# Gate and up of a SwiGLU by Strassen's scheme in seven products, with a fixed order of three engines, and moving operands 256 bytes modulo 512 from weights

## The chip, the core and the metric

The kernel runs on one core of a Trainium2 chip. Times are microseconds (us) of one execution on the device. The kernel before took 1472.33 us, the median of three runs (1470.74 to 1473.45). The engines are TensorE (PE: matmuls; PEld: its weight loads), VectorE (DVE), ScalarE (ACT), GpSimd (POOL) and SyncE (SP, which issues DMAs).

## What is computed

A trunk of two layers over 512 tokens of 1024 features: attention and a SwiGLU feed-forward (FFN) of 2816 hidden features in each, then a last RMS norm. The change is to the two FFNs, cut here to what matters:

```python
def swiglu(h, w_gate, w_up, w_down):
    return (jax.nn.silu(h @ w_gate) * (h @ w_up)) @ w_down

for i in range(DEPTH):
    h = rmsnorm(x, norm_mix[i])
    x = x + attention_i(h)
    h = rmsnorm(x, norm_ffn[i])
    x = x + swiglu(h, w_gate[i], w_up[i], w_down[i])
return rmsnorm(x, norm_final)
```

All of it is float32. A matmul of two float32 operands is made of three fp32r matmuls: each operand is split in a high part (rounded by ACT) and a low part (what is left, by DVE), and high x high, high x low and low x high are added up in PSUM.

## The kernel before

`x` lies in SBUF transposed, features on partitions: 8 tiles (`NK`) of 128 x 512 tokens. `xh` and `xl` are the split input of the stage at hand. Weights come from `wunits`, units of 128 x 1024 floats (512 KB), eight blocks of 128 x 128. `load_unit` issues the DMA on SP into `wraw` and splits it: ACT makes `wh`, DVE makes `wl` (L92, L93). `mm3` (L113 to L119) issues the three products of one block in two halves of 256 tokens, so every matmul has a stationary operand of 128 x 128 and a moving one of 128 x 256: six per block, 48 per unit.

`swiglu` (L495 to L558) runs over 22 hidden blocks f (`NF`). For each, `gate(f)` and `up(f)` are a unit of 48 matmuls each, into PSUM banks `mm`, `sc` and `tp`. `combine(f)` scales both by the RMS norm's row `rb`, applies Silu to the gate, multiplies, and splits the product into `ah[:, f]` and `al[:, f]`. In the first f, `norm_sums` (sums over features, by one-column matmuls) stands between gate and up, and `norm_rows` (transposes into `rrow`, copied to `rb`) behind up. Then the down projection: 8 output blocks j, each of 22 x 6 matmuls with three weight loads. Behind each block comes `residual` (layer 0: adds to `x`, splits the next stage's input, and squares it), or the add, squares and a scaling by GpSimd (layer 1). The last block of layer 1 goes through `final` (L453 to L493): its two token halves are done apart, so that the norm of the first half is worked out while the second half's matmuls run. `sums(0)` is called after 6 of 22 steps of the second half, `leave(0)` after 13.

The order on PE is the order of the program's text (`manual_schedule` for PE). DVE, ACT and the others are put in order by a scheduler. `wpool` holds three sets of weight tiles, so loads run ahead. SBUF addresses come from the pools in order of their tiles. In the program as built, weight tiles start at 0 modulo 512 bytes, and `xh`, `xl`, `ah`, `al`, `oh` and `ol` at 192. In the value projections (PSUM tile `psv`) the roles are exchanged: the weights move and the input is stationary.

Of the kernel before, what the change touches and what calls it, by code (L numbers as in the profile page):

```python
# [14 lines left out]
S = 512  # L15
# [3 lines left out]
H = 16  # L19
# [4 lines left out]
WIN_A = 128  # L24
SLOPES = [float(np.float32(2.0) ** np.float32(-8.0 * (h + 1) / H)) for h in range(H)]
# [39 lines left out]
def trunk(ctx, tc, xT, gains, sink, tabs, qsc, wunits, wv, outT):  # L65
# [6 lines left out]
    spool = ctx.enter_context(tc.tile_pool(name="spool", bufs=2))  # L72
    psum = ctx.enter_context(tc.tile_pool(name="psum", bufs=2, space=bass.MemoryType.PSUM))
# [10 lines left out]
    sink_sb = const.tile([128, H], F32, name="sink_sb")  # L84
# [213 lines left out]
    with tc.tile_pool(name="l0", bufs=2) as pool:  # L298
# [14 lines left out]
        def q_unit(P, i, **kw):  # L313
            def done(ps):
                t = spool.tile([128, S], F32, name="tmp")
                col = 4 * P + i
                nc.vector.scalar_tensor_tensor(t, ps, qs_sb[:, col:col + 1], norm["rb"], op0=OP.mult, op1=OP.mult)
                qk["q", P, i] = [pool.tile([128, S], F32R, name=f"qt{a}", bufs=8) for a in range(2)]
                split_queries(t, qk["q", P, i])
# [131 lines left out]
    def final(product, ps0, ps1, n, j):  # L451
# [42 lines left out]
    def swiglu(u, n):  # L494
        with tc.tile_pool(name="ffn", bufs=2) as pool:  # L495
            ah = pool.tile([128, NF, S], F32R, name="ah", bufs=1)
            al = pool.tile([128, NF, S], F32R, name="al", bufs=1)
            part = {}

            def gate(f):  # L500
                def done(ps):
                    part["g"] = ps
                return unit(u + 2 * f, xh, xl, ("mm", "sc")[f % 2], done)

            def up(f):
                def done(ps):
                    part["u"] = ps
                return unit(u + 2 * f + 1, xh, xl, ("tp", "mm")[f % 2], done)

            def combine(f):  # L510
                gs = pool.tile([128, S], F32, name="gs")
                us = pool.tile([128, S], F32, name="us")
                nc.vector.tensor_tensor(gs, part["g"], norm["rb"], op=OP.mult)
                nc.scalar.activation(gs, gs, AF.Silu)
                nc.vector.tensor_tensor(us, part["u"], norm["rb"], op=OP.mult)
                nc.vector.tensor_tensor(us, us, gs, op=OP.mult)
# [442 lines left out]
```

## Time and profile before

| what | us |
|---|---|
| median of three runs | 1472.33 (1470.74 to 1473.45) |
| the profiled execution's own time | 1473.99 |
| its span | 1472.3 |
| FFN of layer 0 | 187.0 to 547.6 |
| FFN of layer 1 | about 1075 to 1460 |

The profile comes from one execution. A row of a group gives line, engine, operation, output <- inputs, shape and count, then the busy time, the mean duration of one in ns, and the idle time just ahead with what ended it. Matmuls are pipelined: one of 256 columns is recorded with 276 to 290 ns, but starts come closer together. A rate is therefore read from a window's length and count. Rows of a timeline give start, duration, engine, line and operation, and in brackets the idle time ahead. "clock" is the share of its full clock that TensorE was granted.

### The profile page before, as it was taken

To read this page: it belongs to the slowest core of one execution; us is meant where nothing else is said; L and a number is where in the kernel's file an instruction comes from. 1 tells how busy PE (TensorE), PEld (TensorE's weight loads), DVE (VectorE), ACT (ScalarE), POOL (GpSimd) and SP (SyncE) were. 2 spreads that over 40 slices of the span, in tenths; PEclk is the share of its full clock that TensorE was granted. 3 is DMA by queue.
4 is the path that set the end of the run, shared out by engine and by line. 5 is a ranking of instruction groups with operands and counts; after the bars stand their busy time and mean duration, and the time that the engine had idled before them with its cause. 6 is when DMAs were issued, how large, how long until landed. Compare 5 with 4: busy or idle time off the path is not lost.

```text
span 1472.3 us, 29609 instructions
## 1 busy us (share of the span) xinstructions
PE 1453.9 (99%) x12820; PEld 1426.7 (97%) x12820; DVE 732.6 (50%) x1400; ACT 613.9 (42%) x1126; POOL 109.1 (7%) x152
## 2 busy tenths in 40 slices
PE   8999999999999999999999999999999999999997
PEld 8988999999999999999999999999999999999997
DVE  6776544444443345346556556556464444443223
ACT  6776433322323335445545536536343322332221
POOL 3334200000000010000000000000030000000111
PEclk9999999999999999999999999999999999999998
DMA  6110232323223232312212122222132322232331
GB/s 201 58 59 15 87 101 87 101 101 100 94 87 104 94 111 69 101 63 86 79 67 87 58 87 73 72 87 73 44 116 86 101 101 98 90 101 91 96 103 57
DMA packets 38450, 128.29 MB, mean 87 GB/s; under 512 B 4528, under 2 KB 6832, under 8 KB 38320
## 3 DMA queue, kind: packets, MB, share of 16 engines
q1 hardware_dynamic: 36832, 125.08, 25.5%
q8 instruction: 100, 1.64, 0.4%
q10 hardware_dynamic: 1488, 1.33, 0.3%
q14 instruction: 30, 0.25, 0.1%
HBM read 124.29 MB, written 2.10 MB: 86 GB/s over the span
## 4 chain that ended last, share of the span: by engine, by line
PE 94%; DVE 2%; ACT 2%; issue 1%; DMA 0%; POOL 0%; SPq 0%; DVEq 0%; ACTq 0%; POOLq 0%
PE mm L118 51%; PE sc L118 16%; PE psv L118 10%; PE tp L118 8%; PE sc L696 1%; PE sc L637 1%; PE ov L378 1%; PE ov L751 1%; PE sc L140 1%; PE tp L364 1%; PE tp L659 1%; PE ov L678 1%; ACT pr L353 0%; DVE qt L128 0%; PE tp L738 0%
## 5 line engine op out<-in xcount | busy, mean ns | idle before, releaser
L92 ACT ACTIVATE wh<-wraw 128x1024 fp32r<-128x1024 f32 (+3 forms) x239 | 247.6, 1037 | 599.6 <-PE mm L118 252.0
L93 DVE TENSOR_TENSOR wl<-wraw,wh 128x1024 fp32r<-128x1024 f32 (+3 forms) x239 | 290.2, 1215 | 203.3 <-ACT wh L92 202.7
L118 PE MATMUL mm<-xh,wh 128*128 128x256 f32 x1632 | 331.4, 284 | 0.4 <-ACT xh L217 0.4
L118 PE MATMUL mm<-xh,wl 128*128 128x256 f32 x1632 | 321.6, 279 | 2.6 <-DVE wl L93 2.6
L118 PE MATMUL mm<-xl,wh 128*128 128x256 f32 x1632 | 321.7, 279 | 0.7 <-DVE xl L218 0.6
L118 PEld LDWEIGHTS mm<-xh,wh 128*128 128x128 f32 x1632 | 248.5, 189 | 6.3 <-issue 4.8
L118 PEld LDWEIGHTS mm<-xh,wl 128*128 128x128 f32 x1632 | 247.9, 189 | 3.2 <-DVE wl L93 3.2
L118 PEld LDWEIGHTS mm<-xl,wh 128*128 128x128 f32 x1632 | 248.5, 189 | 1.4 <-DVE xl L218 1.3
L232 POOL TENSOR_TENSOR ssum<-ssum,tmp 128x512 f32<-128x512 f32 x34 | 53.7, 1581 | 994.4 <-ACT tmp L228 979.9
L118 PE MATMUL psv<-wh,xh 128*128 128x256 f32 x288 | 82.8, 287 | 0.0
L118 PE MATMUL psv<-wl,xh 128*128 128x256 f32 x288 | 80.4, 279 | 0.0
L118 PE MATMUL psv<-wh,xl 128*128 128x256 f32 x288 | 80.3, 279 | 0.0
L118 PE MATMUL mm<-ah,wh 128*128 128x256 f32 x374 | 74.9, 277 | 0.0
L118 PE MATMUL mm<-al,wh 128*128 128x256 f32 x374 | 74.7, 276 | 0.0
L118 PE MATMUL mm<-ah,wl 128*128 128x256 f32 x374 | 74.7, 276 | 0.0
L118 PE MATMUL tp<-xh,wh 128*128 128x256 f32 x352 | 68.8, 277 | 0.0
L118 PE MATMUL sc<-xh,wh 128*128 128x256 f32 x352 | 68.7, 277 | 0.0
L118 PE MATMUL tp<-xh,wl 128*128 128x256 f32 x352 | 68.6, 276 | 0.0
L118 PE MATMUL tp<-xl,wh 128*128 128x256 f32 x352 | 68.6, 276 | 0.0
L118 PE MATMUL sc<-xh,wl 128*128 128x256 f32 x352 | 68.5, 276 | 0.0
L118 PE MATMUL sc<-xl,wh 128*128 128x256 f32 x352 | 68.5, 276 | 0.0
L118 PE MATMUL sc<-ah,wh 128*128 128x256 f32 x330 | 66.0, 276 | 0.0
(175 smaller groups left out, 2728.6 us busy)
## 6 DMA issues: line engine op xcount, KB each, us to landing
wraw<-wunits SPq DMA_DIRECT2D x192, 512.0 KB, 3.2
wraw<-wv SPq DMA_DIRECT2D x26, 512.0 KB, 3.3
wraw<-wunits SPq DMA_DIRECT2D x16, 384.0 KB, 3.0
x<-xT SPq DMA_DIRECT2D x8, 256.0 KB, 5.1
wraw<-wunits SPq DMA_DIRECT2D x3, 256.0 KB, 5.5
outT<-x ACTq DMA_DIRECT2D x2, 384.0 KB, 2.7
tab<-tabs SPq DMA_DIRECT2D x1, 512.0 KB, 5.5
outT<-x ACTq DMA_DIRECT2D x2, 256.0 KB, 2.2
```

What stands on the lines that cost most here:

```text
L92: nc.scalar.activation(out_h, src, AF.Copy)
L93: nc.vector.tensor_tensor(out_l, src, out_h.bitcast(F32), op=OP.subtract)
L118: nc.tensor.matmul(out[:, cols], a, b[:, cols], start=first and k == 0 and c == 0, stop=last and k == 2, skip_group_check=True)
L140: nc.tensor.matmul(outs[a], qp[a][:, qc], k[a][:, kc], start=first and k is kp, stop=k is low, skip_group_check=True)
L232: nc.gpsimd.tensor_tensor(norm["sum"], norm["sum"], sq, op=OP.add)
L364: nc.tensor.transpose(tp[:, 256 * hf + 128 * i:256 * hf + 128 * i + 128], st["pr"][:, 2 * i + hf, 128 * kb:128 * kb + 128], ident)
L378: nc.tensor.matmul(ov[64 * hf:64 * hf + 64, :256], v0[:, k0 // 128 + kb, vs], st["pt", kb][:, 256 * hf:256 * hf + 256], start=(kb == 0), s ...
L637: nc.tensor.matmul(out, qk["qs", p][a][:, 128 * t:128 * t + 128], kp[k], start=t == ts[0] and k == 0, stop=k == 1, skip_group_check=True)
L659: nc.tensor.transpose(tp[:, (nb * a + kb) * 128:(nb * a + kb) * 128 + 128], st["pr", p, ts][:, a, o + 128 * kb:o + 128 * kb + 128], ident)
L678: nc.tensor.matmul(ov[rows, 128 * t - 64:128 * t + 64], v[:, t - 1 + kb, vs], pt[:, 256 * a + 128 * kb:256 * a + 128 * kb + 128], start=Fa ...
L696: nc.tensor.matmul(ps[a][:, o:o + 128], qk["q", p, 1 + g][rows, cols], qk["k", p, 1 + g][rows, cols], start=(o == 0), stop=True, skip_grou ...
L751: nc.tensor.matmul(ov[rows, 128 * c:128 * c + 128], vals[p // 2, 1 + g][:, c, hv + 64 * a:hv + 64 * a + 64], pts[g][:, 256 * a + 128 * (c ...
```

## The change

The hidden blocks f = 6 to 21 of each FFN no longer take gate and up as two units. The pair is one product of 2 x 2 blocks: the weights are (gate, up) by (first, second half of the features), the input (first, second half of the features) by (first, second half of the tokens). In the Winograd form of Strassen's scheme this takes 7 products of 4 blocks x 3 matmuls, 84 matmuls where there were 96.

- The seven sums of input quarters are built once per FFN (`input_steps`, split into `bh` and `bl`), by DVE and ACT while f = 1 to 5 run in the conventional way (`conventional`, `plain = 6`).
- The sums of weights are built for each pair: two by GpSimd DMAs that add to a tile loaded before (`loads`), two by DVE (`add`). `weights` splits all seven, in tiles `wh`, `wl`, `h57`, `l57`, `h3`, `l3`.
- `strassen` gives a pair's products and what DVE and ACT do with them; `strassens` puts these in slots. A pair starts every seven slots and lasts fifteen. The weights of the next pair are made in seven slots (`MAKE`).
- In these stretches the order of DVE and ACT is that of the text too (`ORDERED`).
- `ah`, `al` hold only three blocks; the rest of the split activations go into `xh`, `xl`, which hold the FFN's input until its use ends. So an FFN runs in parts (`PARTS`): 0 to 11, 11 to 19, 19 to 22 in layer 0, and 0 to 11, 11 to 22 in layer 1, each with its own gate, up and down projection. Slots without a product (in the first pair of a part, and behind its last) are filled with matmuls of the down projection: the last four f of block 7 of the part before, or block 0 of the part itself (`left`).
- `norm_rows` in the first f stands behind five of up's eight steps. In `final` the calls stand after 5 and 11 of 11 steps.
- Tiles named `align`, `align0`, `align1`, `align2`, and `sink_sb`'s new place, shift addresses: weights start at 0 modulo 512 bytes as before, all moving operands of these matmuls at 256, and in `psv` the distance is 256 as well.

```diff
+PARTS = ((0, 11), (11, 19), (19, NF)), ((0, 11), (11, NF))
...
+    spool.tile([128, 16], F32, name="align", bufs=1)
...
+    sink_sb = const.tile([128, H], F32, name="sink_sb")
...
-            if k == 5:
+            if k == 4:
                 run(sums(0))
-            elif k == 12:
+            elif k == 10:
...
-            ah = pool.tile([128, NF, S], F32R, name="ah", bufs=1)
-            al = pool.tile([128, NF, S], F32R, name="al", bufs=1)
+            ah = pool.tile([128, 3, S], F32R, name="ah", bufs=1)
+            al = pool.tile([128, 3, S], F32R, name="al", bufs=1)
...
+            bh = pool.tile([128, 7, 4, 256], F32R, name="bh", bufs=1)
+            bl = pool.tile([128, 7, 4, 256], F32R, name="bl", bufs=1)
+            B11, B21, B22, T1, T2, T3, T4 = range(7)
+            pool.tile([128, 64], F32, name="align2", bufs=1)
...
+            def place(f):
+                if f < 3 or f >= 19:
+                    return ah[:, f % 19, :], al[:, f % 19, :]
+                return xh[:, (f - 3) % 8, :], xl[:, (f - 3) % 8, :]
...
+            def gated(f):
+                part["gs"] = pool.tile([128, S], F32, name="gs")
+                nc.vector.tensor_tensor(part["gs"], part["g"], norm["rb"], op=OP.mult)
+                nc.scalar.activation(part["gs"], part["gs"], AF.Silu)
 
-            def combine(f):
-                gs = pool.tile([128, S], F32, name="gs")
-                us = pool.tile([128, S], F32, name="us")
-                nc.vector.tensor_tensor(gs, part["g"], norm["rb"], op=OP.mult)
-                nc.scalar.activation(gs, gs, AF.Silu)
+            def combined(f):
+                us = part[f] = pool.tile([128, S], F32, name="us", bufs=4)
                 nc.vector.tensor_tensor(us, part["u"], norm["rb"], op=OP.mult)
-                nc.vector.tensor_tensor(us, us, gs, op=OP.mult)
-                split(ah[:, f, :], al[:, f, :], us)
+                nc.vector.tensor_tensor(us, us, part["gs"], op=OP.mult)
+
+            def kept(f):
+                split(*place(f), part[f])
...
+                steps = [lambda j=j: normed(j) for j in range(NK)]
+                steps += [lambda: parts(B11), lambda: less(T1, B11, B12), lambda: parts(B21), lambda: parts(T1),
+                          lambda: less(T2, T1, B22, -1.0), lambda: parts(T2), lambda: less(T3, B22, B12),
+                          lambda: parts(T3), lambda: less(T4, T2, B21, -1.0), lambda: parts(T4), lambda: parts(B22)]
...
+                g, v = wunits[u0 + 2 * f], wunits[u0 + 2 * f + 1]
+                sums = pool.tile([128, 1024], F32, name="w64")
+                nc.sync.dma_start(sums[:, 0:512], g[:, 0:512])
+                nc.sync.dma_start(sums[:, 512:1024], v[:, 512:1024])
+                for k in range(2):
+                    nc.gpsimd.dma_start(sums[:, 512 * k:512 * k + 512], v[:, 0:512], accum_op=OP.add)
+                raw = wpool.tile([128, 1024], F32, name="wraw")
+                nc.sync.dma_start(raw, g)
+                last = pool.tile([128, 512], F32, name="w3")
+                nc.sync.dma_start(last, v[:, 512:1024])
+                return raw, sums, last
...
+                def high(names, home, src):
+                    cols = src.shape[-1]
+                    t[names] = [home[0].tile([128, cols], F32R, name=m) for m in home[1:]]
+                    nc.scalar.activation(t[names][0], src, AF.Copy)
+                    for k, m in enumerate(names):
+                        w[m] = [z[:, 512 * k:512 * k + 512].rearrange("p (j c) -> p j c", j=4) for z in t[names]]
...
+                return w, {"h12": lambda: high((1, 2), (wpool, "wh", "wl"), raw), "l12": lambda: low((1, 2), raw),
+                           "h64": lambda: high((6, 4), (wpool, "wh", "wl"), sums), "l64": lambda: low((6, 4), sums),
+                           "f5": lambda: add(0), "f7": lambda: add(1),
+                           "h57": lambda: high((5, 7), (pool, "h57", "l57"), t["far"]),
+                           "l57": lambda: low((5, 7), t["far"]),
+                           "h3": lambda: high((3,), (pool, "h3", "l3"), last), "l3": lambda: low((3,), last)}
...
+            def product(out, w, k, first):
+                (wh, wl), (xa, xb) = w, (bh[:, k], bl[:, k])
+                for j in range(4):
+                    for i, (a, b) in enumerate(((wh, xa), (wh, xb), (wl, xa))):
+                        nc.tensor.matmul(out, a[:, j], b[:, j], start=first and j == 0 and i == 0,
+                                         stop=j == 3 and i == 2, skip_group_check=True)
...
+                def gate():
+                    nc.vector.tensor_tensor(v["gs"], v["b"], v["gs"], op=OP.add)
+                    nc.scalar.activation(v["gs"], v["gs"], AF.Silu)
+
+                def both():
+                    g, t = v["gs"], v["us"]
+                    nc.vector.scalar_tensor_tensor(t[:, one], v["a"][:, one], -1.0, g[:, one], op0=OP.mult, op1=OP.mult)
+                    nc.vector.scalar_tensor_tensor(t[:, two], t[:, two], -1.0, g[:, two], op0=OP.mult, op1=OP.mult)
+                    nc.scalar.activation(place(f)[0], t, AF.Copy)
+
+                def low():
+                    h, l = place(f)
+                    nc.vector.tensor_tensor(l, v["us"], h.bitcast(F32), op=OP.subtract)
...
+                return ({0: s0, 1: s1, 3: lambda: product(v["a"][:, one], w[5], T2, False),
+                         5: lambda: product(v["b"][:, two], w[4], T1, False),
+                         6: lambda: product(v["a"][:, one], w[6], T3, False),
+                         9: lambda: product(v["a"][:, one], w[3], T4, False),
+                         11: lambda: product(v["b"][:, two], w[7], B22, False)},
+                        {1: lambda: copy("gs", 1, one), 4: lambda: copy("gs", 2, two), 7: lambda: copy("us", 3, two),
+                         8: add, 12: gate, 13: both, 14: low})
+
+
+            MAKE = {0: ("h12",), 1: ("l12",), 2: ("h64", "f5"), 3: ("l64", "h3"), 4: ("l3", "f7"), 5: ("h57",), 6: ("l57",)}
...
+                end = 7 * len(fs) + 8
...
+                        gap = 2
...
+                    for step in work.pop(t, ()):
+                        step()
+                    for step in others.pop(t, ()):
+                        step()
+                    for _ in range(gap):
+                        next(lead if t < 7 else left(), None)
+                    if q == 4 and i + 3 < len(fs):
+                        ready(fs[i + 3], keep=True)
...
-            for f in range(NF):
-                if f == 0:
-                    run(gate(0)[1])
-                    norm_sums()
-                    run(up(0)[1])
-                    norm_rows()
-                else:
-                    run(gate(f)[1])
-                    run(up(f)[1])
-                combine(f)
...
+            ORDERED = {mybir.EngineType.PE, mybir.EngineType.DVE, mybir.EngineType.Activation}
+            plain = 6
+            parts = PARTS[n // 4]
+            run(gate(0)[1])
+            norm_sums()
+            gen = up(0)[1]
+            for _ in range(5):
+                next(gen)
+            norm_rows()
+            run(gen)
+            steps = input_steps()
...
+                gated(0)
+                w = load_unit(wunits[u0 + 2], (NK, 128))
+                for f in range(1, plain):
+                    part["g"] = bank(("mm", "sc")[f % 2])
+                    gen = products(part["g"], w)
+                    for q in range(4):
+                        next(gen), next(gen)
+                        if q == 0:
+                            w = load_unit(wunits[u0 + 2 * f + 1], (NK, 128))
+                            combined(f - 1)
+                        elif q == 2 and f <= 3:
+                            kept(f - 1)
+                        elif q:
+                            make(1)
+                    ps = bank(("tp", "mm")[f % 2])
...
+            for p, (f0, f1) in enumerate(parts):
+                fs = list(range(f0, f1))
...
+                def left():
+                    if not gens:
+                        gens["ps"] = bank("tp")
+                        gens[0] = down(0, fs, at)(gens["ps"], slice(0, S))
+                        gens["early"] = len(fs) - 1
+                    if gens["early"] == 0:
+                        return iter(())
+                    gens["early"] -= 1
+                    return gens[0]
...
+                    if j == NK - 1 and f1 < NF:
+                        first, made = weights(*ready(f1))
+                        for step in made.values():
+                            step()
+                        for _ in range(max(len(fs) - 4, 0)):
+                            next(gen)
+                        lead = gen
+                        continue
...
+        for f0, f1 in PARTS[i]:
+            for b in downs:
+                add([b[:, c:min(c + 8, f1)] for c in range(f0, f1, 8)])
...
+    nc = _bacc.Bacc("TRN2", target_bir_lowering=False, num_devices=1, dynamic_dma_scratch_size=2048)
```

What this does to the order of instructions is shown at three places. First DVE in the run of pairs. Before, one pair f (`gs`, `us`: gate and up; `sc`, `mm`: PSUM):

```order
L513 TENSOR_TENSOR gs<-sc,rb 128x512
L93 TENSOR_TENSOR wl<-wraw,wh 128x1024
L515 TENSOR_TENSOR us<-mm,rb 128x512
L516 TENSOR_TENSOR us<-us,gs 128x512
L93 TENSOR_TENSOR wl<-wraw,wh 128x1024
L93 TENSOR_TENSOR al<-us,ah 128x512
```

The change, seven slots of the steady run (`w_...` are tiles w64, w57 or w3, `h_...` and `l_...` the split parts h57, h3, l57, l3):

```order
L649 TENSOR_TENSOR us<-sc,us 128x256
L606 TENSOR_TENSOR wl<-wraw,wh 128x1024
L612 TENSOR_TENSOR w_3565<-w_3355,wraw 128x512
L606 TENSOR_TENSOR wl<-w_3355,wh 128x1024
L606 TENSOR_TENSOR l_3581<-w_3362,h_3580 128x512
L612 TENSOR_TENSOR w_3565<-w_3565,wraw 128x512
L652 TENSOR_TENSOR gs<-sc,gs 128x512
L657 SCALAR_TENSOR_TENSOR us<-mm,gs 128x256
L658 SCALAR_TENSOR_TENSOR us<-us,gs 128x256
L606 TENSOR_TENSOR l_3613<-w_3565,h_3612 128x1024
L663 TENSOR_TENSOR xl<-us,xh 128x512
```

Six instructions became eleven: a third low part of 1024, one of 512, two weight sums, and the scheme's own adds, while the scalings by `rb` are gone.

Second, PE where gate and up end and block 0 of the down projection follows. Before, the last up unit and then f = 0, 1 and on (`x2`: both token halves):

```order
L118 MATMUL mm<-xh,wh 128x256 x2
L118 MATMUL mm<-xl,wh 128x256 x2
L118 MATMUL mm<-xh,wl 128x256 x2
L118 MATMUL mm<-ah,wh 128x256 x2
L118 MATMUL mm<-al,wh 128x256 x2
L118 MATMUL mm<-ah,wl 128x256 x2
```

The change, at the end of the part of f = 19 to 21, from the last of the seven products (`bh`, `bl` the input sum) to the last f of block 0 and the start of block 1:

```order
L626 MATMUL sc<-bh,h_6092 128x256
L626 MATMUL sc<-bl,h_6092 128x256
L626 MATMUL sc<-bh,l_6093 128x256
L122 MATMUL tp<-ah,wh 128x256 x2
L122 MATMUL tp<-al,wh 128x256 x2
L122 MATMUL tp<-ah,wl 128x256 x2
L122 MATMUL sc<-ah,wh 128x256 x2
```

The activations that `tp` takes here are those of the pair whose last product stands just ahead; before, they were those of f = 0.

Third, ACT at the start of an FFN, from the norm's statistics on (`rb`: the row scale; `wh`: high part of a weight unit). Before:

```order
L249 ACT_TABLE_LOAD
L249 ACTIVATE rstd<-var 128x4
L92 ACTIVATE wh<-wraw 128x1024
L273 ACTIVATE rb<-rrow 128x512
L514 ACT_TABLE_LOAD
L514 ACTIVATE gs<-gs 128x512
L92 ACTIVATE ah<-us 128x512
```

The change:

```order
L253 ACT_TABLE_LOAD
L253 ACTIVATE rstd<-var 128x4
L277 ACTIVATE rb<-rrow 128x512
L532 ACT_TABLE_LOAD
L532 ACTIVATE gs<-gs 128x512
L96 ACTIVATE wh<-wraw 128x1024 x2
L96 ACTIVATE ah<-us 128x512
```

The split of gate 1's weights stood ahead of `rb` and the Silu of gate 0, and now stands behind both.

In the tail, DVE's order before was: statistics of the first token half (`var` to `rstd`), six scalings of that half (L474), the last add (L455), statistics and scalings of the second half. Now the last add stands between the third and the fourth step of the first half's statistics, and the six scalings of the first half between `var` and the reciprocal of the second.

More of the change, by code (lines that the diff above doesn't have):

```diff
@@ new lines, in swiglu, with down, gen @@
+            pairs = {}
+            def down(j, fs, first):
+                def gen(ps, cols):
+                    for k, f in enumerate(fs):
+                        wh, wl = w[k // 8]
+                        h, l = place(f)
+                        mm3(ps[:, cols], wh[:, k % 8], wl[:, k % 8], h[:, cols], l[:, cols], k == 0, k == len(fs) - 1)
+                        yield
+                w = []
+                for c0 in range(0, len(fs), 8):
+                    m = min(8, len(fs) - c0)
+                    w.append(load_unit(wunits[first + j * len(range(0, len(fs), 8)) + c0 // 8][:, :128 * m], (m, 128)))
+                return gen
@@ L557, in trunk @@
+        return at
     u = swiglu(u, 2)
@@ L916, in ffn @@
             add([g[k], u[k]])
[L917 to L918 removed]
+        downs = pack(f["w_down"][i])
+        for f0, f1 in PARTS[i]:
+            for b in downs:
+                add([b[:, c:min(c + 8, f1)] for c in range(f0, f1, 8)])
     ffn(0)
```

184 lines of the change are left out of this document (154 added, 30 removed).

## The prediction

> **What bounds the kernel now.** I read the page first: its engine line, then the chain of work that ended last.
>
> ```profile
> span 1472.3 us, 29609 instructions
> PE 1453.9 (99%) x12820; PEld 1426.7 (97%) x12820; DVE 732.6 (50%) x1400; ACT 613.9 (42%) x1126; POOL 109.1 (7%) x152
> PE 94%; DVE 2%; ACT 2%; issue 1%; DMA 0%; POOL 0%; SPq 0%; DVEq 0%; ACTq 0%; POOLq 0%
> ```
>
> TensorE (PE) is busy for 99% of the span and carries 94% of the chain; VectorE (DVE) and ScalarE (ACT) idle half the time, DMA is nowhere. So time is matmuls times their spacing, plus the few places where PE stops. Next the windows view: length, then each engine's busy time with its instruction count, the granted clock, the DMA share and GB/s. The stretches are the feed-forward stage (FFN) of layer 0, that of layer 1, the out-projection of layer 0, and two seams.
>
> ```profile
> core 0: us, PE busy (x) PEld busy (x) DVE busy (x) ACT busy (x) POOL busy (x), PEclk, DMA share, GB/s
> 187.03:547.60 360.57, 360.57 (x3182) 360.57 (x3181) 153.00 (x178) 112.89 (x133) 11.38 (x7) 1.00 0.29 96
> 1075.00:1453.00 378.00, 378.00 (x3336) 378.00 (x3335) 156.54 (x185) 112.89 (x137) 23.22 (x20) 1.00 0.28 94
> 155.00:185.00 30.00, 30.00 (x257) 30.00 (x256) 19.65 (x21) 15.33 (x21) 10.01 (x6) 1.00 0.34 109
> 555.68:558.88 3.20, 3.20 (x17) 3.20 (x16) 3.20 (x6) 1.78 (x3) 0.00 (x0) 0.50 0.00 0
> 1060.00:1075.00 15.00, 13.75 (x130) 12.87 (x130) 9.35 (x11) 8.60 (x14) 1.94 (x2) 1.00 0.10 35
> ```
>
> In both FFNs PE never stops: 360.57 / 3182 and 378.00 / 3336 are both **113.3 ns** per matmul. The same shape in the out-projection takes 30.00 / 257 = 116.7, so spacing is not fixed by shape. The value projections, by tile (count, durations, first and last start) and by group, are the other end:
>
> ```profile
> L118 PE MATMUL psv<-wh,ol x72: 279/279/279, 574.8 to 599.9; 128*128 128x256 f32 x72
> L118 PE MATMUL psv<-wh,xh 128*128 128x256 f32 x288 | 82.8, 287 | 0.0
> L118 PE MATMUL mm<-xh,wh 128*128 128x256 f32 x768 | 159.5, 289 | 0.0
> ```
>
> 71 steps of three matmuls in 25.1 us are **117.8 ns**, gap-free too. In the program's allocated addresses, weights lie at 0 modulo 512 bytes and moving operands at 192 in the FFN and out-projection (113.3 or 116.7); in psv the roles are exchanged, which makes 320.
>
> **The removed matmuls.** Each of 16 pairs per layer takes 7 products of 12 matmuls instead of 96: 12 x 32 = 384 fewer, 5,952 left in the two FFNs. 384 x 113.3 ns = **-43.5 us**. This holds if nothing else sets the pace of a pair, 84 x 0.1133 = 9.52 us. The other engines' prices, from the groups by shape (count, busy time and mean ns, idle time ahead), and where the mean holds overlap, from the DVE timeline of one pair (start, duration) with the ACT instruction that follows in it:
>
> ```profile
> L93 DVE TENSOR_TENSOR wl<-wraw,wh 128x1024 fp32r<-128x1024 f32 x218 | 269.1, 1235 | 203.0 <-ACT wh L92 202.3
> L583 DVE SCALAR_TENSOR_TENSOR q<-mm,qs_sb,rb 128x512 f32<-128x512 f32 x16 | 12.0, 751 | 23.1 <-PE mm L118 23.1
> L455 DVE TENSOR_TENSOR x<-mm,x 128x256 f32<-128x256 f32 x1 | 0.4, 414 | 0.0
> L92 ACT ACTIVATE wh<-wraw 128x1024 fp32r<-128x1024 f32 x218 | 231.3, 1062 | 550.3 <-PE mm L118 228.2 <-issue 196.2 <-PE sc L118 109.1
> L92 ACT ACTIVATE ah<-us 128x512 fp32r<-128x512 f32 x44 | 27.9, 635 | 30.2 <-DVE us L516 30.2
> L514 ACT ACTIVATE gs<-gs 128x512 f32<-128x512 f32 x44 | 27.1, 616 | 0.2
> L202 ACT ACTIVATE v<-psv,rstd 128x256 f32<-128x256 f32 x36 | 16.4, 469 | 16.5 <-PE psv L118 16.4
> ...
> 340.92 0.69 DVE L515 TENSOR_TENSOR us<-mm,rb 128x512 f32<-128x512 f32 x1 [3.29 <-PE mm L118]
> 341.71 0.69 DVE L516 TENSOR_TENSOR us<-us,gs 128x512 f32<-128x512 f32 x1
> 342.32 1.22 DVE L93 TENSOR_TENSOR wl<-wraw,wh 128x1024 fp32r<-128x1024 f32 x1
> 343.46 0.69 DVE L93 TENSOR_TENSOR al<-us,ah 128x512 fp32r<-128x512 f32 x1
> 342.44 0.64 ACT L92 ACTIVATE ah<-us 128x512 fp32r<-128x512 f32 x1 [0.64 <-DVE us L516]
> ```
>
> The starts show that DVE operations overlap by 0.08: a 1024-wide one occupies 1.14 (342.32 to 343.46), a 512-wide one 0.61 (341.71 to 342.32). By the order, a pair now gives DVE three 1024-wide (l12, l64, l57: 3.42), five 512-wide (f5, f7, l3, gate, low: 3.05), one 256-wide add (0.41 - 0.08 = 0.33) and two 256-wide scaled products (0.751 / 2 each, 0.78 with overhead): 7.58 us; with waits for Silu (0.62) and one handover, 8.4. ACT gets 3 x 1.06 + 0.64 + 3 x 0.47 + 0.62 + 0.64 = 6.5. Both fit in 9.52, so these edits cost nothing while PE covers them; DVE's margin is 1.1 us a pair, and beyond it each us a pair costs 32.
>
> DMA traffic, by the page's list of issues (count, size, us to landing):
>
> ```profile
> wraw<-wunits SPq DMA_DIRECT2D x192, 512.0 KB, 3.2
> ```
>
> Loads grow from 1.05 to 1.79 MB a pair in 9.5 us instead of 10.9. From the share 0.29 that makes about 0.57, or 0.73 if accumulating also reads its target: not full. They are issued some twelve slots (16 us) ahead of use and a load lands in 3.2 us. Two accumulating GpSimd transfers in a row have no row here: taken as two loads of 3.2, cost 0; the other end is a rival below.
>
> **Waits added at FFN start.** The order puts row scale, table load and Silu of gate 0 ahead of the weight split of gate 1. ACT's timeline there, before:
>
> ```profile
> 198.85 1.06 ACT L92 ACTIVATE wh<-wraw 128x1024 fp32r<-128x1024 f32 x1 [3.82 <-issue]
> 199.81 0.58 ACT L273 ACTIVATE rb<-rrow 128x512 f32<-128x512 f32 x1
> 200.41 1.28 ACT L514 ACT_TABLE_LOAD   x1
> 201.80 0.63 ACT L514 ACTIVATE gs<-gs 128x512 f32<-128x512 f32 x1
> ```
>
> Now wh went first and PE waited for nothing. In the new order rb, table, Silu and wh end 0.58 + 1.28 + 0.63 + 1.06 plus handovers, about 3.65 us, behind the row transposes, which have 18 matmuls (2.04) behind them: PE waits 1.6. Its next wait is for wl, 1.14 after wh, with four matmuls (0.45) and a handover between: 0.85 more. Queued behind Silu on ACT are only that split and the next copies. 2 x 2.45 = **+4.9** (0 to 4.9).
>
> **Part ends.** Down block 0 cannot finish until the last pair is split: gate add 0.69, Silu 0.62, two half products 0.39 + 0.47, high part 0.64, low part 0.69, seven handovers of 0.04 (us ends at 342.40, ah starts at 342.44): 3.78 us. By the order, 24 matmuls (2.72) fill this in the three parts of 11, six (0.68) in the part of 8, none in the part of 3. PE stops 3 x 1.06 + 3.10 + 3.78 = **+10.1** (before: 0, all activations were long split).
>
> **The clock behind these stops.** Row 555.68 shows clock 0.50 for 3.20 us, 17 matmuls where 28 fit, 1.3 to 1.4 us lost, behind two microseconds of one-column sums; row 1060 kept 1.00 with a gap of 1.25 us in all (13.75 of 15.00). So stops between 1.25 and about 2 us have no row: the three of 1.06 I take as free, the two over 3 us as 1.4 each, the two of 2.45 as half of that: **+4.2** (0 to 5.6).
>
> [...]
>
> **Seam to layer 1 and tail.** The last part of layer 0 has down blocks of 18 matmuls, 2.04 us, in which DVE must add the residual (0.61), make a 384-wide wl and a low part of the next input:
>
> ```profile
> L93 DVE TENSOR_TENSOR wl<-wraw,wh 128x768 fp32r<-128x768 f32 x16 | 15.3, 959 | 0.1
> L218 DVE SCALAR_TENSOR_TENSOR xl<-x,g_sb,xh 128x512 fp32r<-128x512 f32 x32 | 31.0, 972 | 7.3 <-ACT xh L217 7.3
> ```
>
> 0.61 + 0.48 + 0.97 = 2.06 against 2.04 in each of eight blocks; half a microsecond more in each would be 4. Between 0 and 4, **+1.5**.
>
> The tail, by the timelines of PE and DVE: the last matmul, then the six scalings of the first token half, the add and the statistics of the second.
>
> ```profile
> 1460.02 0.28 PE L118 MATMUL mm<-ah,wl 128*128 128x256 f32 x1
> 1457.65 3.23 DVE L474 TENSOR_TENSOR x<-x,rb 128x256 f32<-128x256 f32 x6 [1.90 <-ACT rb L273]
> 1460.80 0.41 DVE L455 TENSOR_TENSOR x<-mm,x 128x256 f32<-128x256 f32 x1
> 1462.56 0.16 DVE L248 TENSOR_SCALAR var<-ssq 128x2 f32<-128x2 f32 x1 [1.34 <-PE ssq L236]
> 1462.99 0.17 DVE L250 RECIPROCAL rstd<-rstd 128x2 f32<-128x2 f32 x1 [0.27 <-ACT rstd L249]
> ```
>
> Matmuls hid the scalings nearly whole; the add came 0.5 behind the last one (1460.30 to 1460.80). In the new order the first half's statistics end behind that add, so its scalings stand between var and the reciprocal of the second half, with nothing to hide them but ACT's 0.27: 3.23 - 0.5 - 0.27, **+2.5** (0 to 3.2).
>
> **Spacing elsewhere.** Weights stay at 0; every moving operand goes to 256 modulo 512, between the two distances seen. The unknown lies between 113.3 and 117.8, or, nothing excluding it, beyond. In the FFN I take 113.3: nearest in stage and program. Outside: psv has (288 + 128) x 3 = 1,248 matmuls at 117.8, at most 5.6 us to gain; the attention's mm groups (768 x 3 and layer 0's) have about 3,170, at the out-projection's 116.7 at most 10.8. From 0 to -16 I take half, **-8**. [...]
>
> **Sum.** The profiled execution took 1473.99 us by its own time. 1473.99 - 43.5 + 4.9 + 10.1 + 4.2 + 1.5 + 2.5 - 8 = 1445.7. The runs' median, 1472.33, is 1.7 lower: **1444.0**.
>
> **Rivals.**
> - Slower: the new distance acts in the FFN as 320 does in psv. 5,952 x 4.5 ns = 26.8 more, and the 8 not gained: 1444 + 34.8 = **1479**. It decides from (1472.3 - 1452) / 5,952 = 3.4 ns (1452: no gain outside), a spacing of 116.7, just what the out-projection shows at 192. For it: new stops, and slow stretches follow stops. Against: the long FFN rows stay at 113.3. 0.13.
> - Faster: 256 is as far below 113.3 as psv is above. 5,952 x 4.5 = 26.8: **1417**. Against: no row is below 113.3. For: nothing shows 113.3 to be the floor. [...] 0.17.
> - DVE becomes the bound: GpSimd's transfers or late sums stretch its pair from 8.4 to about 10.2: 0.7 x 32 = 22, **1466**. Against: the margin of 1.1. 0.14.
> - It doesn't do what it says: the fixed order of three engines stalls at a slot each pair by 0.9 us, 29 us, **1473**. Against: the busy sums above. 0.06.
>
> **Chances.** The forecast (1435 to 1456, so with a worthless distance too) 0.50, the rivals as given. A measurement can tell about 0.2%, 3 us, from no change. Faster: 0.50 + 0.17 + 0.13 of the third = 0.80; same: 0.05, most of the last; slower: 0.13 and what is left, 0.15. The range runs from the faster rival with a larger gain outside, 1408, to the third with a longer stretch, 1472; beyond it lie the slow spacing and half of the last.
>
> **What would show it.** 32 pairs 9.5 us apart in the new FFN windows, at 113 ns a matmul; ACT's split ending 2 to 3 us behind the last matmul of up 0; PE stops of 1, 3 and 3.8 us ahead of down block 0's last terms, waiting on the low part; clock 0.50 only behind the long ones; psv at less than 117.8. It would be wrong with PE waiting each pair on DVE or on a DMA, or with another spacing in the FFN.

## The result, and the profile after

The changed kernel took **1528.17 us** (median of 4 runs, 1526.59 to 1535.45) against 1472.12 before: 1.039 times as long, 95% interval 1.036 to 1.042. The forecast was 1444, the range ended at 1472. Of the rivals the slower one (1479) had the right sign and, as it turned out, the right place. Of the experiments' runs one alone, of e4_prime, stood apart (1495.6 us at a granted clock of 0.939), and it is left out of that ratio and range.

The page of the changed kernel, the lines that answer to the three shown of before:

```profile
span 1527.7 us, 29626 instructions
PE 1483.0 (97%) x12436; PEld 1449.1 (95%) x12436; DVE 876.3 (57%) x1654; ACT 706.4 (46%) x1316; POOL 167.5 (11%) x216
PE 91%; ACT 3%; DVE 3%; issue 1%; DMA 0%; SPq 0%; DVEq 0%; ACTq 0%
```

384 matmuls fewer, and PE is busy for 29 us more. So the first thing to look at is the spacing. The windows view, in the columns of the prediction: the out-projection, two stretches of Strassen pairs in steady run (layer 0, layer 1), one end of a part, and the seam to layer 1:

```profile
155.00:185.00 30.00, 30.00 (x252) 30.00 (x251) 19.66 (x21) 15.32 (x21) 9.32 (x6) 1.00 0.33 106
270.00:305.00 35.00, 35.00 (x294) 35.00 (x293) 27.02 (x39) 19.73 (x34) 6.96 (x8) 1.00 0.80 195
1345.00:1435.00 90.00, 90.00 (x752) 90.00 (x751) 68.74 (x98) 51.64 (x80) 14.04 (x16) 1.00 0.66 166
308.00:315.00 7.00, 5.06 (x28) 4.65 (x27) 4.06 (x6) 3.32 (x5) 0.00 (x0) 0.76 0.34 107
570.00:590.00 20.00, 15.39 (x97) 14.62 (x97) 18.35 (x24) 14.29 (x19) 7.72 (x7) 0.83 0.30 104
```

In 90 us of pairs PE never stops, and 752 matmuls are one per 119.7 ns. (A window also counts the matmuls that its two edges cut, so short windows read low; from start to start it is 120.0, nearly without exception.) Before it was 113.3. At 84 matmuls a pair takes 10.05 us, and VectorE is busy for 68.74 / (90 / 10.05) = 7.7 us of it, so it is not VectorE that paces the pairs. The last two rows show the other part of the loss: PE stops, and a clock below 1.00 behind them.

From the starts of the norm sums, which both kernels have in every FFN, the 55.4 us of span fall as follows:

| from, to | before, us | after, us | difference |
|---|---|---|---|
| start, sums of FFN 0 | 192.5 | 193.4 | +0.9 |
| sums of FFN 0, sums of layer 1 | 360.4 | 388.5 | +28.1 |
| sums of layer 1, sums of FFN 1 | 550.8 | 563.6 | +12.8 |
| sums of FFN 1, last matmul | 356.4 | 367.7 | +11.3 |
| last matmul, end | 12.3 | 14.6 | +2.3 |

### The profile page after: what moved, and what is told of

It is laid out like the page before. It is cut to its first block, busy times and chain, and to the rows that moved or that the text cites. A ratio compares the mean times of both kernels' runs of the same rounds, so it can differ in the third digit from the quotient of the medians.

```text
span 1527.7 us, 29626 instructions
## 1 busy us (share of the span) xinstructions
PE 1483.0 (97%) x12436; PEld 1449.1 (95%) x12436; DVE 876.3 (57%) x1654; ACT 706.4 (46%) x1316; POOL 167.5 (11%) x216
## 4 chain that ended last, share of the span: by engine, by line
PE 91%; ACT 3%; DVE 3%; issue 1%; DMA 0%; SPq 0%; DVEq 0%; ACTq 0%
PE mm L122 38%; PE mm L626 12%; PE sc L122 10%; PE psv L122 9%; PE sc L626 9%; PE tp L122 4%; PE ov L384 1%; PE sc L144 1%; PE tp L370 1%; PE sc L1009 1%; PE sc L950 1%; PE ov L1064 1%; DVE wl L97 1%; PE tp L972 1%; PE ov L991 1%
## 5 line engine op out<-in xcount | busy, mean ns | idle before, releaser
L96 ACT ACTIVATE wh<-wraw 128x1024 fp32r<-128x1024 f32 (+3 forms) x191 | 179.9, 950 | 265.1 <-PE mm L122 154.5
L97 DVE TENSOR_TENSOR wl<-wraw,wh 128x1024 fp32r<-128x1024 f32 (+3 forms) x191 | 214.7, 1128 | 147.0 <-ACT wh L96 146.1
L626 PE MATMUL mm<-bh,h 128*128 128x256 f32 x256 | 73.1, 285 | 1.6 <-ACT gs L638 1.6
L626 PE MATMUL mm<-bh,wh 128*128 128x256 f32 x256 | 72.9, 285 | 1.3 <-ACT gs L638 1.3
L606 DVE TENSOR_TENSOR l<-w,h 128x512 fp32r<-128x512 f32 (+1 forms) x64 | 61.1, 955 | 21.2 <-ACT h L600 21.2
L626 PE MATMUL sc<-bh,wh 128*128 128x256 f32 x256 | 72.4, 283 | 0.0
L626 PE MATMUL sc<-bl,wh 128*128 128x256 f32 x256 | 72.4, 283 | 0.0
L626 PE MATMUL mm<-bl,h 128*128 128x256 f32 x256 | 72.4, 283 | 0.0
L626 PE MATMUL sc<-bh,wl 128*128 128x256 f32 x256 | 72.4, 283 | 0.0
L626 PE MATMUL mm<-bh,l 128*128 128x256 f32 x256 | 72.4, 283 | 0.0
```

The lines of the kernel that those rows point to most:

```text
L96: nc.scalar.activation(out_h, src, AF.Copy)
L97: nc.vector.tensor_tensor(out_l, src, out_h.bitcast(F32), op=OP.subtract)
L606: nc.vector.tensor_tensor(l, src, h.bitcast(F32), op=OP.subtract)
L626: nc.tensor.matmul(out, a[:, j], b[:, j], start=first and j == 0 and i == 0, stop=j == 3 and i == 2, skip_group_check=True)
```

## Experiments: the distance

**p1_distance: TensorE alone.** A kernel of its own, in which nothing else runs: the gate's pattern of matmuls, 192 to a series, with only the moving operand's address changed from series to series. The rest of the network is left out.

```diff
+    for d in range(0, 512, 32):
+        series(f"up{d:03d}", 0, d // 4)
+    for d in range(480, -1, -32):
+        series(f"dn{d:03d}", 0, d // 4)
+    for d in range(0, 512, 64):
+        series(f"gp{d:03d}", 0, d // 4, gap=True)
```

> TensorE alone: series of 192 matmuls as the gate's (three products, two halves of 256 columns) with the moving operand 0, 32, ... 480 bytes modulo 512 behind the weights, going up, then down, then every 64 with one-column matmuls ahead; the rest of the network is left out. Theory A (the distance sets the spacing): the series at 256 start every 120.0 ns in all three passes, as the changed kernel's did; those at 192 every 113.3 to 118, those at 320 every 117.8. Rival B (what the other engines and transfers do beside TensorE sets it): every series at one spacing, near 113, as nothing else runs. A third, C: 256 has two phases like 192 and the changed kernel only sat in the slower: then 256 reads 113 in one pass and 120 in another.

Two pieces of its PE timeline, three successive rows each of two matmuls with the same weights: the series at 192 and the series at 256, both behind one-column matmuls.

```profile
845.12 0.39 PE L102 MATMUL gp<-xh,wl 128*128 128x256 f32 x2
845.35 0.39 PE L102 MATMUL gp<-xh,wh 128*128 128x256 f32 x2
845.58 0.39 PE L102 MATMUL gp<-xl,wh 128*128 128x256 f32 x2
...
873.00 0.40 PE L102 MATMUL gp<-xh,wl 128*128 128x256 f32 x2
873.24 0.40 PE L102 MATMUL gp<-xh,wh 128*128 128x256 f32 x2
873.48 0.40 PE L102 MATMUL gp<-xl,wh 128*128 128x256 f32 x2
```

A step of two matmuls is 0.227 us at 192 and 0.240 at 256. All series, by the mean from start to start in their second half (ns):

| distance, bytes | up | down | behind a gap |
|---|---|---|---|
| 0 and 256 | 120.0, 120.0 | 120.0, 120.0 | 120.0, 120.0 |
| 32 and 288 | 117.8, 117.8 | 116.7, 116.7 | |
| 64 and 320 | 117.8, 117.8 | 117.8, 113.3 | 117.8, 117.8 |
| 96 and 352 | 120.0, 120.0 | 120.0, 120.0 | |
| 128 and 384 | 118.7, 118.7 | 118.7, 118.7 | 118.7, 120.0 |
| 160 and 416 | 117.3, 117.3 | 118.7, 117.3 | |
| 192 and 448 | 117.8, 117.8 | 117.8, 113.3 | 113.3, 117.8 |
| 224 and 480 | 118.3, 118.3 | 118.3, 118.3 | |

Going up, each distance reads as the one 256 bytes further on: the period is **256 bytes**, and 256 is 0 again, the slowest of the multiples of 64, and one value in all passes. Only 64 and 192 modulo 256 ever reach 113.3, and each of them also shows 117.8. Two more series, at 192 with the weights themselves moved by 128 and 256 bytes, took 117.8 both. That alone can't tell the distance from the moving operand's own address, since these lay at 64 and 192 modulo 256, which read alike. The value projections of the kernel before can: their moving operand lay at 0, as in the series at 0, but beside an input at 192, and they took 117.8 and not 120.0. Theory A holds; B and C fall.

**p2_fine: near 192.** The same in steps of 4 bytes.

```diff
+    for d in range(164, 224, 4):
+        series(f"up{d:03d}", 0, d // 4)
+    for d in range(220, 160, -4):
+        series(f"dn{d:03d}", 0, d // 4)
+    for d in range(176, 209, 4):
+        series(f"gp{d:03d}", 0, d // 4, gap=True)
```

> As p1_distance, but distances 164 to 220 in steps of 4 bytes, up and down, and 176 to 208 behind one-column matmuls. Theory: 113.3 ns is to be had only close to 192 (64 modulo 128), and each distance there has both phases. Rival: some distance beside 192 holds 113.3 in all passes, so that a shift by a few bytes would take the slow phase out of every stage.

At 192 all three passes were 113.3. At 188 they were 120.0, 116.7 and 120.0, at 196 123.4, 120.0 and 120.0, and no other distance from 164 to 220 came below 116.7. So, in steps of 4 bytes, 113.3 is not a valley round 192, it is the single point. No distance was found that has only the fast phase over both runs. What chooses the phase is not known: in p1 a run straight into 192 was slow both times, in p2, which ran on another chip, it was fast both times.

**e1_before_256: the distance without Strassen.** The kernel before, with these lines alone:

```diff
+    spool.tile([128, 16], F32, name="align", bufs=1)
...
+    sink_sb = const.tile([128, H], F32, name="sink_sb")
     xh = const.tile([128, NK, S], F32R, name="xh")
...
-    sink_sb = const.tile([128, H], F32, name="sink_sb")
```

> The kernel before with nothing but its moving operands shifted from 192 to 256 bytes modulo 512 (conventional gate and up). Theory A: the feed-forward stages at 120.0 ns instead of 113.3, 6,336 x 6.7 = 42 us, and attention some 14 us as in the changed kernel: about 1528 us. Rival B: 113.3 and 1472 us.

1526.79 us (1526.64 to 1527.29), 1.037 times the kernel before, interval 1.036 to 1.039. Its window in the FFN of layer 1:

```profile
1160.00:1500.00 340.00, 340.00 (x2836) 340.00 (x2835) 128.94 (x148) 90.48 (x108) 12.40 (x13) 1.00 0.27 88
```

340 / 2836 = 119.9 ns without a stop, with conventional gate and up and the old share of DMA. The span grew by 52.8 us: 6,336 x 6.7 = 42.4 in the FFNs and 10.4 outside them.

**e2_after_192: Strassen without the distance.** The changed kernel with `align`, `align0`, `align1` and the move of `sink_sb` taken back, and this line to keep the weights at 0:

```diff
-            pool.tile([128, 64], F32, name="align2", bufs=1)
+            pool.tile([128, 80], F32, name="align2", bufs=1)
```

> The changed kernel with its moving operands back at 192 modulo 512, weights at 0, all else kept. Theory A: 113.3 ns in most of the gap-free stretches, 5,952 x 6.7 = 40 us and some 14 us outside less than the change: about 1475 us, so what Strassen saves (43.5) is all taken by PE stops and half clock. Rival B: 120 stays, 1528 us. If the slow phase of 192 (117 to 118) holds behind the new stops, up to 25 us more than 1475.

1489.77 us (1485.9 to 1493.78), 1.012 (1.010 to 1.014). The distance alone is worth 38.4 us here, some 15 less than theory A's 53. In part that is because 192 has two phases: the FFN's matmuls outside of stops and half clock took 114.6 ns in the mean, not 113.3, which is 8 us over 5,952, and long stretches ran at 117.8. The remaining 7 us were not worked out. Two stretches of its trace without a stop, one in each phase:

```profile
1307.00:1401.00 94.00, 94.00 (x832) 94.00 (x831) 72.91 (x104) 53.77 (x86) 14.01 (x16) 1.00 0.68 170
1418.00:1468.00 50.00, 50.00 (x427) 50.00 (x426) 15.53 (x19) 13.18 (x19) 14.94 (x13) 1.00 0.20 69
```

And without the distance Strassen is still 1.2% slower than the kernel before. Much of the rest lies in the stops.

## Experiments: the stops

Two places of the changed kernel. At the start of FFN 0, gate 1's first matmuls (the bracket is the idle time ahead, and the instruction that ended it):

```profile
202.05 0.51 PE L122 MATMUL sc<-xh,wh 128*128 128x256 f32 x2 [1.43 <-ACT wh L96]
203.31 0.51 PE L122 MATMUL sc<-xh,wl 128*128 128x256 f32 x2 [0.52 <-DVE wl L97]
```

At the end of the first part, behind the next to last product: the first matmuls of down block 0, which were meant to fill a gap, then what ACT and DVE do there.

```profile
308.62 0.28 PE L626 MATMUL mm<-bh,wl 128*128 128x256 f32 x1
310.32 0.50 PE L122 MATMUL tp<-ah,wh 128*128 128x256 f32 x2 [1.42 <-ACT wh L96]
310.66 0.40 PE L122 MATMUL tp<-al,wh 128*128 128x256 f32 x2
311.58 0.70 PE L122 MATMUL tp<-ah,wl 128*128 128x256 f32 x2 [0.52 <-DVE wl L97]
312.08 0.63 PE L122 MATMUL tp<-ah,wh 128*128 128x256 f32 x2
...
309.21 2.41 ACT L96 ACTIVATE wh<-wraw 128x1024 fp32r<-128x1024 f32 x3
...
310.30 1.70 DVE L97 TENSOR_TENSOR wl<-wraw,wh 128x1024 fp32r<-128x1024 f32 x2 [0.70 <-ACT wh L96]
```

The fill's own weights are late: `left` calls `load_unit` in the slot in which its first matmul stands, and in the fixed order ACT comes to that split only then (309.21). From one start to the next, 308.62 to 310.32 is 1.70 and 310.77 to 311.58 about 0.80, that is 2.3 us over the spacing. It happens in four parts, and for 1.05 in the short one. The matmuls from 312.08 on last 0.63 a pair: half clock (0.50 granted from 312 to 315).

**e3_start: only the first place.** From here on the operands are at 192, as in e2, but for e6.

```diff
+            w1 = load_unit(wunits[u0 + 2], (NK, 128))
             norm_rows()
...
-                w = load_unit(wunits[u0 + 2], (NK, 128))
+                w = w1
```

> The changed kernel at distance 192 with one part changed: the weights of gate 1 are loaded and split ahead of the row scale and Silu of gate 0, as in the kernel before. Theory: the two PE stops at the start of each feed-forward stage (1.8 and 0.8 us, by the profile of the kernel at 192) go, 2 x 2.4 = 4.7 us and some half clock behind them: 1489.8 becomes about 1484. Rival: something else is late in their place (the row scale for gate 0's bank, or the table load) and the time stays at 1490.

1476.12 us (1474.8 to 1478.75), 1.0026 (1.0015 to 1.0037). The two stops are gone from its trace, as the theory had it. But the gain on e2 is 13.7, not 5: matmuls of FFN 0 outside of stops and half clock came down from 114.8 to 113.6 ns, 3.5 us, and the rest is spread over several stages. (e2 ran on another chip than e3 to e5; the kernel before took 1472.4 on both.)

**e4_prime: only the second place.** Block 0's weights are loaded and split ahead, by two functions made of what `left` did:

```diff
+                    if t == 7 * len(fs) - 9:
+                        fetch()
+                    if t == 7 * len(fs) - 4:
+                        prime()
```

> The changed kernel at distance 192 with one other part changed: the weights of the down projection's block 0 are loaded nine slots and split four slots ahead of the last pair's end, and no longer where its first matmuls stand. Theory: the stops there (1.7 and 0.8 us in four parts, 1.2 in the short one) were the weight split, so 10 us and some half clock go: about 1478. Rival: they were the last pair's own chain of gate, Silu, product and split; then the stops stay and the time stays near 1490.

1470.45 us (1466.71 to 1472.25), 0.9975 (0.9965 to 0.9986): 19.3 less than e2 where 12 were expected. The stops at block 0's first matmuls are gone in all five parts, so they were the weight split and not the last pair's chain. In FFN 1 half clock went too: of 49 matmuls that in e2 started some 0.21 us after the one ahead, 16 were left.

**e5_all: both, and the fill moved.** Of the slots without a product behind the last pair, only the first keeps its fill; what it had elsewhere follows the last product:

```diff
+                    if t >= 7 * len(fs) and t != 7 * len(fs):
+                        gap = 0
                     for _ in range(gap):
```

> Both edits, and most of the fill of a part's end moved behind the last of the seven products (two of its steps stay ahead). Theory: PE is left with the stop of the three-long part (about 3 us) and the seam to the next layer; 15 us of stops and most of the half clock of the feed-forward stages go, and fewer stops leave more matmuls in the 113.3 phase: 1462 to 1472, thus at or below the kernel before. Rival: the slow phase of 117.8 holds all the same, so that only the stops go: 1474 or more.

**1458.96 us** (1456.12 to 1463.55), 0.9909 (0.9886 to 0.9932): less than both kernels, by 0.9% and 4.5%. Its page, and behind it a window of steady pairs in layer 1:

```profile
span 1454.4 us, 29640 instructions
PE 1421.5 (98%) x12436; PEld 1389.3 (96%) x12436; DVE 876.3 (60%) x1654; ACT 702.7 (48%) x1316; POOL 168.8 (12%) x216
```

The window:

```profile
1300.00:1375.00 75.00, 75.00 (x664) 75.00 (x664) 59.00 (x85) 44.29 (x71) 10.58 (x12) 1.00 0.66 166
```

664 in 75 us is 113.0 (113.3 without the edges' matmuls). From the sums of FFN 1 to the last matmul it takes 337.6 us instead of 356.4: 18.7 of the 21.8 that 192 matmuls less are worth. FFN 0 gains only 4.3 (356.1 instead of 360.4 to the sums of layer 1), by the three-long part and the seam.

**e6_stops_at_256: the same three edits at the change's own distance.**

> The changed kernel at its own distance, 256, with the three edits of e5_all (gate 1's split earlier, block 0's weights earlier, fill behind the last product). At 256 no phase can change, so this prices the stops alone. By the changed kernel's trace they are 2 x 2.3 at the starts, 4 x 2.3 + 1 at block 0's weights, about 2.5 at the last low part and some 5 of half clock, 22 us: about 1506. Rival: of the 31 us between 1489.8 and 1459.0 at 192 all were the stops' own time: then 1497. A saving well below 22 us would say that most of it at 192 was the phase that stops leave behind.

1502.9 us (1502.66 to 1503.73), 1.021 (1.0195 to 1.0226): 25.3 us less than the changed kernel, where 22 were expected. Only one phase was seen at 256, so this is the price of those stops and their half clock. At 192 the same edits gave 30.8; the other 5.5 are what I take to be matmuls in the fast phase that fewer stops leave undisturbed. e2's mean of 114.6 against e5's 113.4 over 5,952 matmuls, 7.1 us, is of that size.

**e7_seam: who is late at the seam to layer 1.** e5_all without the low part of the down weights of layer 0's last part, blocks 1 to 7:

```diff
+            nc.scalar.activation(tiles[1][:, cols], tiles[0][:, cols], AF.Copy)
+            return chunks(tiles, shape)[:1] * 2
```

> e5_all without the low part of the down weights of layer 0's last part (blocks 1 to 7 use the high part in its place; TensorE does the same matmuls, VectorE 7 x 0.48 us less). Theory: VectorE is what is late at the seam to layer 1, so the stops there (1.3, 1.5 and 2.6 us) shrink by about 3.4 us, and with them some half clock: 1453 to 1456. Rival: ScalarE's high part or GpSimd's sum is late there; then 1459 stays.

1457.44 us (1455.65 to 1457.94) against 1458.96 (1456.12 to 1463.55): no difference that these runs can tell, and not the 3 to 6 us expected. What PE waited for at the seam in e5_all, by the view of waits (total, times, longest):

```profile
PE mm L121 <- DVE xl L221: 2.4, 1, 2.4
PE mm L121 <- ACT xh L220: 1.3, 1, 1.3
PE mm L121 <- DVE wl L96: 1.2, 1, 1.2
PE sc L121 <- DVE wl L96: 0.4, 1, 0.4
```

The same in e7_seam:

```profile
PE mm L126 <- DVE xl L226: 2.3, 1, 2.3
PE mm L126 <- ACT wh L95: 1.2, 1, 1.2
PE mm L126 <- DVE wl L96: 1.1, 1, 1.1
```

One wait went to ScalarE, and the longest, for the low part of the next input, stayed. So that one share of VectorE's work is not the cause. The timelines of VectorE and ScalarE in e7_seam show what took its place:

```profile
529.35 0.68 DVE L288 TENSOR_TENSOR x<-sc,x 128x512 f32<-128x512 f32 x1
531.29 1.12 DVE L226 SCALAR_TENSOR_TENSOR xl<-x,g_sb,xh 128x512 fp32r<-128x512 f32 x1 [1.26 <-ACT xh L225]
532.34 0.67 DVE L288 TENSOR_TENSOR x<-mm,x 128x512 f32<-128x512 f32 x1
...
530.06 1.20 ACT L225 ACTIVATE xh<-x,g_sb 128x512 fp32r<-128x512 f32 x1 [0.87 <-DVE x L288]
```

From one residual add to the next it is still 2.99 us (3.00 to 3.05 in e5_all): VectorE now idles 1.26 for ScalarE's high part, and its next add stands behind the low part that needs it. So at the first blocks it is this chain that sets the pace: add, high part, low part. The longest wait is another matter. In the changed kernel's trace VectorE has three low parts of the next layer's other operand ahead of the one waited for (576.61, 2.47 us, shown below), which would explain why it stays; an order that puts them behind wasn't tried, so this is read from the trace and not shown.

## Why the prediction was wrong

The terms of the sum against what the changed kernel's trace and e1 show (stops are starts beyond the spacing, added up):

| term | predicted, us | found, us |
|---|---|---|
| 384 matmuls, at 113.3 ns | -43.5 | -43.5 |
| spacing in the FFNs | 0 | +39.9 (5,952 x 6.7) |
| spacing outside | -8 | +10.4 (e1) |
| gate 1's weights at FFN start | +4.9 | +4.5 (2 x 2.27) |
| block 0's weights | none | +10.1 (4 x 2.26 + 1.05) |
| the last pair's chain at part ends | +10.1 | +8.6 |
| first products waiting for copies of PSUM | none | +4.1 |
| half clock, and single slow starts beside stops | +4.2 | +11.2 |
| seam to layer 1, with its half clock | +1.5 | +6.4 |
| tail | +2.5 | +2.3 |

The found terms add up to 54.0 of 55.4.

**The step that failed is "Spacing elsewhere"**: "The unknown lies between 113.3 and 117.8, or, nothing excluding it, beyond. In the FFN I take 113.3: nearest in stage and program." It took the distance for a scale on which 256 lies "between the two distances seen", and gave the "beyond" no price above 117.8. The runs show that the spacing has a period of 256, with 113.3 at single points; 256 stands with 0 and takes 120.0. That is +39.9 us in the FFNs where 0 was set, and +10.4 outside them where -8 was. The trace of before had rows at distance 0, which I didn't use: the score matmuls of layer 0, whose keys and queries, by the sizes of the tiles, lie at the same place modulo 512.

```profile
54.04 0.28 PE L140 MATMUL sc<-kt,qt 128*128 128x256 f32 x1
54.16 0.28 PE L140 MATMUL sc<-kl,qt 128*128 128x256 f32 x1
54.28 0.28 PE L140 MATMUL sc<-kt,qt 128*128 128x256 f32 x1
54.40 0.28 PE L140 MATMUL sc<-kl,qt 128*128 128x256 f32 x1
```

They start every 0.12 us. So 120 was there as a bound, and with it in the FFNs alone the range would have reached 1444 + 40. The slower rival had the cause, priced it at 4.5 ns where 6.7 were due, and took the attention's 8 us as merely not gained. One thing that it had in its favour, slow stretches behind stops, is no rule: behind the stop of before at 1070.3 (1.06 us from start to start) 282 matmuls are 113.4 ns apart. The faster rival, a spacing below 113.3, showed at none of the distances tried. p1 has TensorE alone, one shape, clock 1.00 (windows 200 to 215 and 866 to 874), and 113.3 to 120.0 ns by address only: where weights and moving operands lie to each other does set the spacing here. By what mechanism, no run shows.

**The stops were sized at half.** The ones that I worked out came true: the start of the FFN, the three-long part (3.9 against 3.78), the eight-long (2.8 against 3.10), the tail. The one missed is in the order of the text: I counted the 24 matmuls of the fill as cover, and didn't ask where the fill's own weights are split. The rest of this error is the clock. I had it follow the stops over 3 us, and at half price those of 2.45. The trace has half clock for 3.4 us behind pairs of stops of 1.7 and 0.8 us at three part ends of 11 and at the eight-long one (clock 0.76 in the window 308 to 315 above), and not behind the same pair at the start of the FFN, nor behind the eight-long part's stop of 2.5. It is no fixed rule: e3 has such a pair at a part end without half clock, and e4 one at the start of FFN 0 with it. The pair at the start of FFN 0 in the changed kernel, the part end in e3, the start of FFN 0 in e4:

```profile
201.00:208.00 7.00, 5.43 (x43) 5.23 (x44) 5.94 (x10) 3.53 (x5) 0.00 (x0) 1.00 0.45 146
301.00:308.00 7.00, 6.07 (x50) 5.86 (x51) 3.16 (x4) 1.72 (x3) 0.00 (x0) 1.00 0.39 131
200.50:207.50 7.00, 5.83 (x34) 5.62 (x35) 6.33 (x10) 3.12 (x4) 0.00 (x0) 0.76 0.46 149
```

Over the changed kernel, e2, e3 and e4 it came behind 11 of 12 such pairs at part ends and 1 of 6 at FFN starts; what decides is not known. The two stops make 2.5 us together, with four matmuls between them.

**The seam** I priced by a 384-wide low part at 0.48 and a steady 2.06 per block. In the changed kernel's timeline of DVE and ACT it goes

```profile
566.50 0.69 DVE L284 TENSOR_TENSOR x<-mm,x 128x512 f32<-128x512 f32 x1
567.10 1.02 DVE L97 TENSOR_TENSOR wl<-wraw,wh 128x384 fp32r<-128x384 f32 x1
568.48 1.14 DVE L222 SCALAR_TENSOR_TENSOR xl<-x,g_sb,xh 128x512 fp32r<-128x512 f32 x1 [0.36 <-ACT xh L221]
569.53 0.68 DVE L284 TENSOR_TENSOR x<-sc,x 128x512 f32<-128x512 f32 x1
...
576.61 2.47 DVE L222 SCALAR_TENSOR_TENSOR ol<-x,g_sb,oh 128x512 fp32r<-128x512 f32 x3
...
567.22 1.22 ACT L221 ACTIVATE xh<-x,g_sb 128x512 fp32r<-128x512 f32 x1 [0.86 <-DVE x L284]
```

with 3.03 us from one residual add to the next: the weights' low part takes 1.02, and VectorE then still waits for ScalarE, whose high part takes 1.22. My sum left that high part out, though the low part of the input needs it, and the trace of before had its 1.20 us at this very place:

```profile
548.99 1.20 ACT L217 ACTIVATE xh<-x,g_sb 128x512 fp32r<-128x512 f32 x1
```

By e7 it is this wait, and not the size of the weights' low part, that holds the pace.

**What was right**: 84 matmuls in a pair with VectorE under them (7.7 us busy, 7.58 forecast), transfers hidden (DMA share 0.66 in the steady run of layer 1, 0.57 to 0.73 forecast; 0.80 in layer 0's first part), and accumulating GpSimd transfers in time. The rivals of a slow VectorE and of a stall at each pair are out. With the stops mended and the operands at 192, Strassen's scheme gains 0.9%, a third of its 43.5 us.

## What to carry to other kernels

Before an address is argued about, put TensorE alone in a small kernel and sweep the distance of moving operands to weights: here it cost 1 ms of chip time and was worth 53 us, more than the algorithm. Don't interpolate between two distances; look for rows at any others that the trace has. And where work is to fill a gap, follow its operands too: a fill whose weights are split in the slot that it fills is a new stop (2.3 us here, in four parts).

## What the hardware showed

- Gap-free matmuls of one shape (fp32r, 128 x 128 weights, 256 columns) started every 113.3 to 123.4 ns with nothing changed but where the moving operand lies against the weights; the sweep going up had a period of 256 bytes. 4 bytes off 192, 113.3 becomes 116.7 to 123.4. Many distances have more than one value (188 has 116.7 and 120.0); 0 has 120.0 only.
- At 64 and 192 there are two phases, 113.3 and 117.8; a phase lasts through thousands of gap-free matmuls (the kernel before held 113.3 over 3,118 of them, from 199.4 to 552.8 us). In e2's FFNs it changed only across stops or slow starts (two of 0.22 us at 275 were enough), and not at each of them. This can make small edits look larger than they are: e3 took away 4.7 us of stops and gained 13.7.
- Half clock, 3.4 us of it, came behind two stops that together made 2.5 us, with four matmuls between them: in 11 of 12 places of one kind and 1 of 6 of another.
